# The order of seven products and their PSUM banks in a two-layer decoder trunk

## The chip, the cores and the metric

One core of a Trainium2 chip runs the whole program. The metric is the device time of one execution in microseconds; lower is better. TensorE (PE) multiplies, VectorE (DVE) and ScalarE (ACT) prepare its operands and read its results, SyncE (SP) issues plain loads from HBM, GpSimd (POOL) issues loads that add onto what is in SBUF.

## The reference

Two decoder layers over 256 tokens of width 2048, in float32. Each layer is a mixer and a feed-forward part:

```python
for layer in range(DEPTH):
    h = rms_norm(x, norm_mix[layer])
    x = x + (swa_ssd_mixer(h, ...) if layer % 2 == 0 else dilated_mixer(h, ...))
    h = rms_norm(x, norm_ffn[layer])
    x = x + squared_relu_mlp(h, w_up[layer], w_down[layer])

def squared_relu_mlp(h, w_up, w_down):
    u = jnp.einsum('bsd,df->bsf', h, w_up)
    return jnp.einsum('bsf,fd->bsd', jnp.square(jax.nn.relu(u)), w_down)
```

The change lies in the second product of the feed-forward part: `u` is 256 x 8192, `w_down` is 8192 x 2048, and there are two such layers.

## The kernel before

**Precision and pieces.** Each weight tile of 2 x 128 rows and 512 columns is loaded by SyncE, rounded into a high part by ScalarE (`whi`) and a low part by VectorE (`wlo`), and multiplied three times: activations high by weights high, high by low, low by high. The unit of the plan is a *piece*, one such tile. A piece of `w_up` is 12 matmuls of 512 columns, since both halves of the tokens (t = 0, 1) use it; a piece of the seven products is 6.

**The order of work** is a list of pieces, `plan`, which `run` walks. At piece i it issues the low part of piece i + 2, the load of piece i + 6, the high part of piece i + 3 and the weight sum of piece i + 4 (in this order), then the reads of the banks that the piece before has finished, then some steps of side tasks (norms, transposes, operands), and then piece i's matmuls. Every engine does its own instructions in the order in which they are issued. There are four buffers for low parts and five for high parts, so the low part of a piece waits until the piece four places back has left TensorE. Loads of `w_up` go through four tiles (`wraw`).

**Stages.** The 16 units of `w_up` (512 columns, 8 pieces each) come in order. Of `u`, 1024 columns make one stage c, 0 to 7. Stages 0 to 6 multiply by `w_down` in two *sets* of seven products each: set j = 0 makes output columns 0 to 1023, set j = 2 columns 1024 to 2047. Stage 7 is plain (`down`), four units of four pieces. `mixed` puts a stage's 28 product pieces between the pieces of `w_up` of the stages that follow: 18, 17, 17, 18, 17, 17 and 8 of them for stages 0 to 6. In stage 6 the first nine product pieces go with the last 8 pieces of `w_up`, the other 19 between the pieces of stage 7.

**The seven products.** A set takes a 2 x 2 block of token halves and `w_down` row halves by a 2 x 2 block of weights (names "11", "12", "21", "22": row half, column half) and computes it with 7 products instead of 8, as in Strassen's and Winograd's method. Each product has two pieces, h = 0 and 1. P1 and P2 use operands as they are (`uhl`, or `uh` and `ul`), the others sums of operands (`sh`, `sl`, `uh`). Their weights are a block or a sum of blocks:

- "12" is loaded with P1, and GpSimd's DMA adds block 22 onto it (`accumulate`); Q7 uses it.
- "11" is loaded with P1; when P1's low part is made, GpSimd's DMA adds block 12 onto it; Q5 uses it.
- "21" and "22" are loaded with P2; Q3 uses "22" as it is.
- Q6 uses the sum of "11" and "22", which VectorE adds into a tile of its own, "t2". Q4 uses "21" plus t2, added into the tile of "21".

The products of a set are added up in three PSUM banks, which come from a pool of four (`aux`, tile `sp`; the transposes and other small things use the same four): `a`, `b`, `c`. A later product on a bank adds onto the earlier ones, which is how the method shares its sums. After each product `evict` lets VectorE add or subtract the bank's content to or from a 128 x 512 block of the result, `res`. A product that adds onto a bank must wait until the read of the product before it on that bank has ended.

The lines: `SEVEN`, `LOADS` and `SUMS` at 238 to 241; `Seven.fetch` (load, L260), `Seven.add` (the sum), `Seven.accumulate` (L274), `Seven.evict`; `run` with its `low`, `high`, `add`, `fetch`. Since all vector, scalar and matmul operations go through one recording helper, the profile gives them line L71.

Of the kernel before, what the change touches and what calls it, by code (L numbers as in the profile page):

```python
# [11 lines left out]
OP = mybir.AluOpType  # L12
# [28 lines left out]
def trunk(ctx: ExitStack, tc: tile.TileContext, x, norm_mix, norm_ffn, w_up, w_down, ab_w_in, ab_q_norm,  # L41
# [33 lines left out]
    V, S, PE = Engine(nc.vector, "V", 90, 1.04), Engine(nc.scalar, "S", 240, 0.83), Engine(nc.tensor, "PE", 0, 0.84)  # L75
# [157 lines left out]
    def unit(*a, **k):  # L233
# [1 line left out]

    SEVEN = (("P1", "a", "11"), ("P2", "b", "21"), ("Q7", "c", "12"), ("Q6", "a", "t2"), ("Q5", "a", "11"),
             ("Q4", "c", "21"), ("Q3", "a", "22"))
    LOADS = {"P1": ("12", "11"), "P2": ("21", "22")}  # L240
    SUMS = {"Q6": ("t2", "11", "22"), "Q4": ("21", "21", "t2")}

    class Seven:

# [12 lines left out]
        def fetch(self, p, h):  # L257
            for b in LOADS.get(SEVEN[p][0], ()):
                r, c = self.rows[int(b[0]) - 1] + h * KC, self.c0 + (int(b[1]) - 1) * W
                nc.sync.dma_start(self.tile(b, h),  # L260
                                  self.w[r * 128:(r + KC) * 128, c:c + W].rearrange("(k p) c -> p k c", p=128))
                if b == "12":
                    self.accumulate("12", 1, h)

        def add(self, p, h):
            if SEVEN[p][0] in SUMS:
                o, x, y = SUMS[SEVEN[p][0]]
                x, y = self.raw[x, h], self.raw[y, h]
                V.tensor_tensor(self.raw[o, h] if o != "t2" else self.tile(o, h), x, y, op=OP.add)

        def accumulate(self, b, half, h):

# [5 lines left out]
        def source(self, p, h):  # L278
            return self.raw[SEVEN[p][2], h]

        def evict(self, p):

            name, b, _ = SEVEN[p]
            t, j, op = {"P1": (0, 0, OP.add), "P2": (0, 0, OP.add), "Q6": (1, 0, OP.add), "Q7": (1, 1, OP.subtract),
                        "Q5": (1, 1, OP.subtract), "Q4": (1, 0, OP.add), "Q3": (0, 1, OP.subtract)}[name]
            r = self.to[t][j]
            V.tensor_tensor(r, r, self.bank[b], op=op)
            if p == 6 and self.after is not None:
                self.after()

    def run():
# [60 lines left out]
        for i, (u, c) in enumerate(todo):  # L352
            if i:
                low(i + AHEAD - 1)
                fetch(i + AHEAD - 1 + RAW)
                high(i + AHEAD)
                add(i + AHEAD + 1)
# [4 lines left out]
            if isinstance(u, Seven):  # L362
                p, h = c
                name, b, _ = SEVEN[p]
                if p in u.needs and h == 0:
# [837 lines left out]
```

## Time and profile before

| | us |
|---|---|
| median of 3 runs | 2362.49 (2360.01 to 2366.78) |
| profiled execution | 2363.23, its span 2361.4 |
| busy PE / DVE / ACT / POOL | 2282.4 / 1794.7 / 1302.3 / 143.3 |
| mean granted clock of TensorE | 0.982 |
| moved by DMA | 483.49 MB, 205 GB/s in the mean |

The feed-forward stages with sets stand at about 535 to 1210 us and 1665 to 2355 us of the span. A view by stretches gives for each window of time the busy time of each engine, the number of its instructions (x), the clock that TensorE was granted (1.00 is full), the DMA engines' busy share and GB/s. A row of waits reads: engine, tile and line of the waiting instruction, whom it waited for, total us, times, longest us. A row of the timeline reads: start, length, engine, line, operation with its output and inputs, and in brackets the idle time ahead and what ended it. A matmul's length in the timeline (0.39 us) is its way through the array; back to back, they start 0.23 us apart.

### The profile page before, as it was taken

Reading aid. Unit: us, or ns where it says so; the run is one execution under the profiler, and the core shown is the slowest. Engines: PE = TensorE matmul, PEld = TensorE weight load, DVE = VectorE, ACT = ScalarE, POOL = GpSimd, SP = SyncE. Lnnn points to the kernel's source line nnn. Section 1 sums busy time; section 2 is a strip of 40 time slices with the busy share of each in tenths; the row PEclk is TensorE's granted clock in tenths of the full one; section 3 lists DMA queues with packets and bytes.
Section 4 is the critical chain, followed back from the end, with each engine's and each line's share of the span. In section 5 each row is a group of like instructions: output and inputs, shape, how many; then the busy total and the mean of one; then the engine's idle time right before and its main releaser. Section 6 shows DMA issues by size and latency. Waiting matters only on the chain.

```text
span 2361.4 us, 30348 instructions
## 1 busy us (share of the span) xinstructions
PE 2282.4 (97%) x10981; PEld 1886.5 (80%) x10981; DVE 1794.7 (76%) x2534; ACT 1302.3 (55%) x1639; POOL 143.3 (6%) x132
## 2 busy tenths in 40 slices
PE   8999999999999999999899999999999999999989
PEld 7999988887877877878688778778787787877867
DVE  6779886557887877978786767655687797877877
ACT  5565554445565655655565555554565565655654
POOL 1000000001001010011000000000101001101100
PEclk9999999999999999999999999999999999999999
DMA  7546555569778697697746555446879769688784
GB/s 228 165 137 195 177 177 187 187 198 274 191 229 252 196 273 208 193 294 202 225 147 191 160 160 170 156 160 186 254 203 278 205 198 270 198 245 240 207 248 125
DMA packets 259959, 483.49 MB, mean 205 GB/s; under 512 B 17444, under 2 KB 28240, under 8 KB 259808
## 3 DMA queue, kind: packets, MB, share of 16 engines
q1 hardware_dynamic: 219264, 416.34, 53.7%
q0 software_dynamic: 30976, 58.87, 14.0%
q10 hardware_dynamic: 9568, 6.34, 0.9%
q8 instruction: 86, 1.41, 0.2%
q14 instruction: 65, 0.53, 0.1%
HBM read 479.36 MB, written 2.13 MB: 204 GB/s over the span
## 4 chain that ended last, share of the span: by engine, by line
PE 79%; DMA 15%; DVE 3%; ACT 2%; issue 1%; SPq 0%; ACTq 0%; DVEq 0%
PE acc L71 55%; PE sp L71 19%; DMA wraw<-in_w_up_dram 11%; DMA sraw<-in_w_down_dram 4%; DVE wlo L71 1%; PE sc L71 1%; PE uT L71 1%; ACT whi L71 1%; PE o L71 1%; PE pT L71 1%; PE yp L71 1%; PE xT L71 0%; DMA wraw<-in_ab_w_in_dram 0%; DVE res L71 0%; DVE sraw L71 0%
## 5 line engine op out<-in xcount | busy, mean ns | idle before, releaser
L71 DVE TENSOR_TENSOR wlo<-wraw,whi 128x1024 fp32r<-128x1024 f32 (+1 forms) x568 | 687.8, 1215 | 259.8 <-PE acc L71 150.3
L71 ACT ACTIVATE whi<-wraw 128x1024 fp32r<-128x1024 f32 (+1 forms) x568 | 597.1, 1053 | 456.2 <-PE acc L71 273.8
L71 PE MATMUL acc<-whi,hThi 128*128 128x512 f32 (+1 forms) x1632 | 657.8, 403 | 21.2 <-ACT whi L71 19.7
L71 PE MATMUL acc<-wlo,hThi 128*128 128x512 f32 (+1 forms) x1632 | 644.8, 395 | 14.2 <-DVE wlo L71 14.0
L71 ACT ACTIVATE whi<-sraw 128x1024 fp32r<-128x1024 f32 x392 | 412.2, 1058 | 424.9 <-DVE sraw L71 137.5
L71 PE MATMUL acc<-whi,hTlo 128*128 128x512 f32 (+1 forms) x1632 | 642.9, 394 | 0.6 <-DVE hTlo L71 0.6
L71 DVE TENSOR_TENSOR wlo<-sraw,whi 128x1024 fp32r<-128x1024 f32 x392 | 476.1, 1223 | 128.7 <-ACT whi L71 65.7
L71 PEld LDWEIGHTS acc<-whi,hThi 128*128 128x128 f32 x1632 | 312.6, 192 | 91.2 <-ACT whi L71 23.8
L71 PEld LDWEIGHTS acc<-wlo,hThi 128*128 128x128 f32 x1632 | 313.0, 192 | 79.6 <-DVE wlo L71 18.6
L71 PEld LDWEIGHTS acc<-whi,hTlo 128*128 128x128 f32 x1632 | 312.8, 192 | 66.6 <-DVE hTlo L71 1.2
L274 POOL DMA_DIRECT2D sraw<-in_w_down_dram x112 | 134.8, 1204 | 2162.0 <-DMA sraw<-in_w_down_dram 1038.4
L71 PE MATMUL sp<-whi,sh 128*128 128x512 f32 x448 | 176.8, 395 | 8.7 <-DVE res L71 8.7
L71 PE MATMUL sp<-wlo,sh 128*128 128x512 f32 x448 | 176.4, 394 | 1.1 <-DVE wlo L71 1.1
L71 PE MATMUL sp<-whi,sl 128*128 128x512 f32 x448 | 176.1, 393 | 0.0
L71 DVE TENSOR_TENSOR res<-res,sp 128x512 f32<-128x512 f32 x196 | 134.1, 684 | 26.7 <-PE sp L71 26.4
L71 DVE TENSOR_TENSOR sraw<-sraw 128x1024 f32<-128x1024 f32 x112 | 136.7, 1220 | 0.0
L71 PE MATMUL acc<-hThi,whi 128*128 128x256 f32 x384 | 112.4, 293 | 0.0
L71 PE MATMUL acc<-hThi,wlo 128*128 128x256 f32 x384 | 108.6, 283 | 0.0
L71 PE MATMUL acc<-hTlo,whi 128*128 128x256 f32 x384 | 108.5, 283 | 0.0
L71 PEld LDWEIGHTS sp<-whi,sh 128*128 128x128 f32 x448 | 85.7, 191 | 28.1 <-ACT whi L71 9.1
L71 PEld LDWEIGHTS sp<-wlo,sh 128*128 128x128 f32 x448 | 85.4, 191 | 19.8 <-DVE wlo L71 1.9
L71 PEld LDWEIGHTS sp<-whi,sl 128*128 128x128 f32 x448 | 85.2, 190 | 18.0
(227 smaller groups left out, 2708.6 us busy)
## 6 DMA issues: line engine op xcount, KB each, us to landing
wraw<-in_w_up_dram SPq DMA_DIRECT2D x256, 512.0 KB, 5.1
sraw<-in_w_down_dram SPq DMA_DIRECT2D x224, 512.0 KB, 8.8
sraw<-in_w_down_dram POOLq DMA_DIRECT2D x112, 512.0 KB, 9.9
wraw<-in_ab_w_in_dram SPq DMA_DIRECT2D x96, 512.0 KB, 3.7
wraw<-in_c_w_qkv_dram SPq DMA_DIRECT2D x96, 512.0 KB, 4.1
wraw<-in_ab_w_out_dram SPq DMA_DIRECT2D x48, 512.0 KB, 3.5
wraw<-in_w_down_dram SPq DMA_DIRECT2D x32, 512.0 KB, 4.3
wraw<-in_c_w_o_dram SPq DMA_DIRECT2D x32, 512.0 KB, 3.5
```

The source lines that it names most:

```text
L71: return f(out, *a, **k)
L274: nc.gpsimd.dma_start(self.raw[b, h], self.w[r * 128:(r + KC) * 128, c:c + W].rearrange("(k p) c -> p k c", p=128), accum_op=OP.add)
```

## The change

Q3 moves from the seventh place to the third, and gets a bank `d` of its own. The order was P1, P2, Q7, Q6, Q5, Q4, Q3 and is P1, P2, Q3, Q7, Q6, Q5, Q4. Because Q3 no longer adds onto bank `a`, Q5's content of `a` is now read twice, into two blocks of `res`. And since "22" has been used by then, the sum for Q6 is written into the tile of "22" instead of a tile of its own; Q4's sum reads it there.

```diff
-    SEVEN = (("P1", "a", "11"), ("P2", "b", "21"), ("Q7", "c", "12"), ("Q6", "a", "t2"), ("Q5", "a", "11"),
-             ("Q4", "c", "21"), ("Q3", "a", "22"))
+    SEVEN = (("P1", "a", "11"), ("P2", "b", "21"), ("Q3", "d", "22"), ("Q7", "c", "12"), ("Q6", "a", "22"),
+             ("Q5", "a", "11"), ("Q4", "c", "21"))
     LOADS = {"P1": ("12", "11"), "P2": ("21", "22")}
-    SUMS = {"Q6": ("t2", "11", "22"), "Q4": ("21", "21", "t2")}
+    SUMS = {"Q6": ("22", "11", "22"), "Q4": ("21", "21", "22")}
...
-                V.tensor_tensor(self.raw[o, h] if o != "t2" else self.tile(o, h), x, y, op=OP.add)
+                V.tensor_tensor(self.raw[o, h], x, y, op=OP.add)
...
-            t, j, op = {"P1": (0, 0, OP.add), "P2": (0, 0, OP.add), "Q6": (1, 0, OP.add), "Q7": (1, 1, OP.subtract),
-                        "Q5": (1, 1, OP.subtract), "Q4": (1, 0, OP.add), "Q3": (0, 1, OP.subtract)}[name]
-            r = self.to[t][j]
-            V.tensor_tensor(r, r, self.bank[b], op=op)
+            for t, j, op in {"P1": ((0, 0, OP.add),), "P2": ((0, 0, OP.add),), "Q6": ((1, 0, OP.add),),
+                             "Q7": ((1, 1, OP.subtract),), "Q4": ((1, 0, OP.add),), "Q3": ((0, 1, OP.subtract),),
+                             "Q5": ((1, 1, OP.subtract), (0, 1, OP.subtract))}[name]:
+                r = self.to[t][j]
+                V.tensor_tensor(r, r, self.bank[b], op=op)
```

How the order of instructions moves, at three places. TensorE, layer 0, stage 1, first set, where the fifth product ends and the sixth begins with no piece of `w_up` between them (`sp_` with a number is one bank's tile, `whi` and `wlo` the weights' parts, `sh` and `sl` or `uh` and `ul` the operands). Before, Q5's last three matmuls and Q4's first three:

```order
L71 MATMUL sp_6111<-whi_6255,sh_6068 128x512
L71 MATMUL sp_6111<-wlo_6264,sh_6068 128x512
L71 MATMUL sp_6111<-whi_6255,sl_6069 128x512
L71 MATMUL sp_6200<-whi_6266,uh_6017 128x512
L71 MATMUL sp_6200<-wlo_6287,uh_6017 128x512
L71 MATMUL sp_6200<-whi_6266,ul_6018 128x512
```

Now, Q6's last three and Q5's first three:

```order
L71 MATMUL sp_6111<-whi_6254,sh_6068 128x512
L71 MATMUL sp_6111<-wlo_6262,sh_6068 128x512
L71 MATMUL sp_6111<-whi_6254,sl_6069 128x512
L71 MATMUL sp_6111<-whi_6264,sh_6068 128x512
L71 MATMUL sp_6111<-wlo_6285,sh_6068 128x512
L71 MATMUL sp_6111<-whi_6264,sl_6069 128x512
```

Both products now write the same bank, and the read of the first lies between them.

VectorE at the same place (`wlo<-sraw` is a product piece's low part, `wlo<-wraw` that of a piece of `w_up`, `sraw<-sraw` a sum of blocks, `res<-res,sp` the read of a bank). Before, up to Q5's read of `sp_6111`:

```order
L71 TENSOR_TENSOR wlo_6253<-sraw_5970,whi_6245 128x1024
L71 TENSOR_TENSOR sraw_6035<-sraw_6035,sraw_6174 128x1024
L71 TENSOR_TENSOR wlo_6264<-sraw_5985,whi_6255 128x1024
L71 TENSOR_TENSOR res_82<-res_82,sp_6111 128x512
L71 TENSOR_TENSOR wlo_6287<-sraw_6035,whi_6266 128x1024
L71 TENSOR_TENSOR sraw_6062<-sraw_6062,sraw_6198 128x1024
L71 TENSOR_TENSOR wlo_6300<-wraw_6243,whi_6291 128x1024
L71 TENSOR_TENSOR wlo_6310<-sraw_6062,whi_6302 128x1024
L71 TENSOR_TENSOR res_82<-res_82,sp_6111 128x512
```

Now, up to Q6's read of `sp_6111`:

```order
L71 TENSOR_TENSOR wlo_6262<-sraw_6064,whi_6254 128x1024
L71 TENSOR_TENSOR res_82<-res_82,sp_6245 128x512
L71 TENSOR_TENSOR wlo_6285<-sraw_5970,whi_6264 128x1024
L71 TENSOR_TENSOR wlo_6297<-wraw_6240,whi_6289 128x1024
L71 TENSOR_TENSOR sraw_6035<-sraw_6035,sraw_6037 128x1024
L71 TENSOR_TENSOR wlo_6308<-sraw_5985,whi_6299 128x1024
L71 TENSOR_TENSOR res_82<-res_82,sp_6111 128x512
```

Ahead of the last read there were a low part, a sum, a low part of `w_up` and a low part; now the sum stands behind the low part of `w_up`.

TensorE, layer 0, stage 6, first set, where several product pieces follow each other. Before, the end of Q6's second piece and the beginning of Q5's first, on one bank:

```order
L71 MATMUL sp_9700<-whi_9820,sh_9671 128x512
L71 MATMUL sp_9700<-wlo_9829,sh_9671 128x512
L71 MATMUL sp_9700<-whi_9820,sl_9672 128x512
L71 MATMUL sp_9700<-whi_9831,sh_9671 128x512
L71 MATMUL sp_9700<-wlo_9839,sh_9671 128x512
L71 MATMUL sp_9700<-whi_9831,sl_9672 128x512
```

Now, the same place in the row of pieces, the end of Q7's second piece and the beginning of Q6's first:

```order
L71 MATMUL sp_9844<-whi_9816,sh_9673 128x512
L71 MATMUL sp_9844<-wlo_9826,sh_9673 128x512
L71 MATMUL sp_9844<-whi_9816,sl_9674 128x512
L71 MATMUL sp_9700<-whi_9828,sh_9671 128x512
L71 MATMUL sp_9700<-wlo_9837,sh_9671 128x512
L71 MATMUL sp_9700<-whi_9828,sl_9672 128x512
```

Q6 and Q5 are parted there by a piece of stage 7 now, and the two products that touch are on two banks.

## The prediction

> **What bounds the kernel now.** I read the shares of the engines first, then the stretches of 60 us, then the waits of TensorE, then the timeline at the places of the waits. Of the page:
>
> ```profile
> PE 2282.4 (97%) x10981; PEld 1886.5 (80%) x10981; DVE 1794.7 (76%) x2534; ACT 1302.3 (55%) x1639; POOL 143.3 (6%) x132
> ```
>
> TensorE is busy for 97% of the span, so what a change can win is its 79 us of idle time (2361.4 - 2282.4) and what goes with it. The view of stretches says where that lies (length, then busy time and instructions of each engine, the granted clock, the DMA share, GB/s):
>
> ```profile
> 660.00:720.00 60.00, 60.00 (x274) 49.70 (x273) 53.92 (x53) 37.48 (x40) 4.82 (x4) 1.00 0.68 191
> 720.00:780.00 60.00, 55.93 (x232) 44.70 (x231) 45.89 (x46) 32.00 (x35) 8.42 (x7) 0.91 0.97 288
> 1260.00:1320.00 60.00, 60.00 (x299) 47.64 (x298) 38.60 (x104) 32.21 (x46) 0.00 (x0) 1.00 0.52 166
> ```
>
> Outside the feed-forward stages TensorE never stops. Inside them full stretches alternate with stretches in which the DMA engines are 97% busy, TensorE loses 4 us and its clock falls. So TensorE is the bound everywhere, and once in each stage the loads are. The timeline of stage 2's first set (start, length, engine, operation; in brackets the idle time before it and what ended it):
>
> ```profile
> 743.80 1.06 ACT L71 ACTIVATE whi<-sraw 128x1024 fp32r<-128x1024 f32 x1 [6.93 <-DMA sraw<-in_w_down_dram]
> 744.91 0.73 PE L71 MATMUL sp<-whi,uh 128*128 128x512 f32 x1 [2.06 <-ACT whi L71]
> 746.17 0.79 PE L71 MATMUL sp<-wlo,uh 128*128 128x512 f32 x1 [0.53 <-DVE wlo L71]
> 748.35 1.06 ACT L71 ACTIVATE whi<-wraw 128x1024 fp32r<-128x1024 f32 x1 [3.50 <-DMA wraw<-in_w_up_dram]
> ```
>
> The matmul that waits has `uh` as its operand: of the first two products that is P2, the second. ScalarE waits for P2's second weight tile, and then for the next tile of `w_up`, which stands behind it in SyncE's queue. The same pair of waits stands once in every stage, at P2 and the `w_up` piece behind it. Of the waits of TensorE:
>
> ```profile
> PE acc L71 <- ACT whi L71: 19.7, 8, 3.8
> PE acc L71 <- DVE wlo L71: 14.0, 11, 4.0
> PE sp L71 <- DVE res L71: 8.7, 3, 4.2
> PE sp L71 <- DVE wlo L71: 7.9, 13, 0.8
> PE sp L71 <- ACT whi L71: 7.4, 4, 2.8
> ```
>
> The third row is the one that this change touches: a product that adds onto a bank waits until VectorE has read the product before it out of that bank.
>
> **The change part by part.** The loads first. P1 and P2 stay in front, they fetch the same tiles at the same pieces, and the accumulating DMAs are issued at the same pieces: SyncE's and GpSimd's queues hold the same transfers in the same order. So the pair of waits at P2 stays, and I count nothing for it. What is won is time for the sums, and that nobody waited for:
>
> ```profile
> L71 DVE TENSOR_TENSOR sraw<-sraw 128x1024 f32<-128x1024 f32 x112 | 136.7, 1220 | 0.0
> L71 DVE TENSOR_TENSOR res<-res,sp 128x512 f32<-128x512 f32 x196 | 134.1, 684 | 26.7 <-PE sp L71 26.4
> ```
>
> The 112 sums had 0.0 us of idle time before them, so the accumulated tiles had always landed. Their number and size stay; only the tile that they write is another.
>
> Each set reads a bank once more, since Q3's block now takes Q5's bank too: 28 x 0.684 = 19 us more of VectorE. It hides: in the full stretch 660 to 720 VectorE is busy 53.92 of 60 us, which leaves 6.1 us where some 1.4 sets add about 1 us. Were VectorE the bound for all of the sets, it would cost the 19 us. The fourth bank comes from the same four buffers as before; Q3's bank is free again after its one read, at most two banks are held for long, as before, and I count nothing.
>
> The order of the banks is what costs. Bank `a` takes P1, Q6, Q5 and then Q3 before, and P1, Q6, Q5 now. Q6 and Q5 follow each other in both. What parts them is the plan: a unit of `w_up` (12 matmuls) mostly stands between two products, but in stages 1, 2, 4 and 5 the fifth and sixth product of the first set touch. Before these were Q5 and Q4, on banks `a` and `c`; now they are Q6 and Q5, both on `a`. The instructions of TensorE show it as 18 matmuls in a row on one bank, four times a layer, and in stage 6's second set the same pair touches once more: 10 new places. What leaves is the pair in stage 6's first set, 24 matmuls in a row, once a layer.
>
> What one new place costs is read where the fifth product ends today, in stage 1 (DVE from 669, PE's first matmul of the fifth product's two pieces and of the sixth):
>
> ```profile
> 670.74 1.22 DVE L71 TENSOR_TENSOR wlo<-sraw,whi 128x1024 fp32r<-128x1024 f32 x1
> 671.88 1.22 DVE L71 TENSOR_TENSOR sraw<-sraw 128x1024 f32<-128x1024 f32 x1
> 672.38 0.39 PE L71 MATMUL sp<-whi,sh 128*128 128x512 f32 x1
> 673.01 1.22 DVE L71 TENSOR_TENSOR wlo<-wraw,whi 128x1024 fp32r<-128x1024 f32 x1
> 673.74 0.39 PE L71 MATMUL sp<-whi,sh 128*128 128x512 f32 x1
> 674.31 1.22 DVE L71 TENSOR_TENSOR wlo<-sraw,whi 128x1024 fp32r<-128x1024 f32 x1
> 675.10 0.39 PE L71 MATMUL sp<-whi,uh 128*128 128x512 f32 x1
> 675.45 0.68 DVE L71 TENSOR_TENSOR res<-res,sp 128x512 f32<-128x512 f32 x1
> ```
>
> The read of the bank ended at 676.13 (675.45 + 0.68), and the next product began at 675.10. On one bank it would have begun 0.14 us behind the read (that gap is in the stage 6 rows below), at 676.27: a wait of 1.2 us. Now one sum moves. Before it stood ahead of the `w_up` piece's low part (671.88); in the changed order it stands behind it. That low part can't begin before TensorE is through with the `w_up` piece four pieces back, at about 672.55 (its last matmul, one spacing of 0.23 before 672.38, lasts 0.39), for there are four buffers. So: low part 672.55, sum 1.14 later at 673.7, low part at 674.8, the read at 675.95 to 676.64, the next product at 676.8. That is 1.7 us behind 675.10. The eight such places cost 13.6 us. In stage 6's second set the low part and the sum both stand between the release and the read, with 6 matmuls instead of 12 to cover them: the unit ahead is through, then 1.14 + 1.14 + 0.69 + 0.14 = 3.1 us with 1.2 us of matmuls, a wait of 2.0 us, twice: 4.0 us. Behind the waiting matmul stands all of TensorE's work, nothing overtakes it. The wait's bounds: 1.2 us if the sum finds a gap, 5.9 us (4.2 and a half-clock stretch) if VectorE is as far behind as in stage 6. I take the worked value, for at 675 VectorE was not behind. The ten together: 17.6 us, between 12 and 59.
>
> Stage 6's first set, as it is now:
>
> ```profile
> 1126.99 1.22 DVE L71 TENSOR_TENSOR wlo<-sraw,whi 128x1024 fp32r<-128x1024 f32 x1
> 1129.75 0.39 PE L71 MATMUL sp<-whi,sh 128*128 128x512 f32 x1
> 1135.80 0.39 PE L71 MATMUL sp<-whi,sl 128*128 128x512 f32 x1
> 1139.53 0.69 DVE L71 TENSOR_TENSOR res<-res,sp 128x512 f32<-128x512 f32 x1
> 1140.36 0.47 PE L71 MATMUL sp<-whi,sh 128*128 128x512 f32 x1 [4.18 <-DVE res L71]
> 1143.81 1.25 ACT L71 ACTIVATE relu<-acc,rs 128x512 f32<-128x512 f32 x2
> 1147.77 0.79 PE L71 MATMUL acc<-whi,uh 128*128 128x512 f32 x1 [1.68 <-ACT uh L71]
> ```
>
> (1139.53 + 0.69 = 1140.22, and TensorE went on at 1140.36: the 0.14.) Six pieces run here without a unit between them, and the wait of 4.18 us lies inside. The changed set puts Q3, Q7 and Q6 there, on three banks, so that wait goes. What is late next is VectorE itself: six low parts, two sums and two reads from 1126.99 on, 8 x 1.14 + 2 x 0.6 = 10.3, so the last low part is done at 1137.3, and TensorE ends the six pieces at about 1138.4 instead of 1144.8 (1140.36 and the 12 matmuls that were left, 8 of them at half clock). Then the first piece of the last stage needs `uh`, whose chain starts with ScalarE's `relu`. That stands behind a high part which waits for a buffer of the first Q6 piece, leaves TensorE at 1137, and has two more ahead of it: `relu` at about 1139.5. From `relu` to the first matmul it took 3.96 us (1147.77 - 1143.81), so 1143.4 instead of 1147.77: 4.3 us won a layer, 8.6 in all, between 0 (the chain starts where it does now) and 11.8 (the wait and its half-clock stretch, both layers).
>
> Sum: 13.6 + 4.0 - 8.6 = +9.0 us on the profiled execution's 2363.23 us, 2372.2. The median of the runs shown is 0.7 us below that execution, so I say 2371.
>
> [...] The stretches around such waits (660.50 to 664 and 1152 to 1156 are full speed for comparison):
>
> ```profile
> 655.50:659.00 3.50, 3.04 (x7) 2.09 (x7) 3.50 (x4) 3.50 (x5) 0.00 (x0) 0.50 0.61 170
> 660.50:664.00 3.50, 3.50 (x19) 2.90 (x19) 3.43 (x4) 1.69 (x3) 1.20 (x1) 1.00 0.87 273
> 1140.90:1144.30 3.40, 3.40 (x10) 2.62 (x9) 2.75 (x3) 1.45 (x2) 0.00 (x0) 0.51 0.86 260
> 1148.50:1151.00 2.50, 2.46 (x7) 1.58 (x6) 2.50 (x3) 1.11 (x2) 0.00 (x0) 0.50 0.98 262
> ```
>
> Behind the waits of 2.19 us (655), 4.18 us (1140) and 1.68 us (1147, with short transposes ahead of it) the clock is half for some 3.4 us, which costs 1.7 us. Behind two waits just before the first of them it was not:
>
> ```profile
> 651.55 0.50 PE L71 MATMUL sp<-wlo,uh 128*128 128x512 f32 x1 [0.76 <-DVE wlo L71]
> 651.88 0.40 PE L71 MATMUL sp<-whi,ul 128*128 128x512 f32 x1
> 652.12 0.39 PE L71 MATMUL sp<-whi,uh 128*128 128x512 f32 x1
> ```
>
> There the matmuls go on at the full spacing of 0.23 us. A new wait of 1.7 us between dense matmuls lies between these rows, and I count no half clock. [...]
>
> **The rivals.**
>
> No net change, 2363 (0.26): VectorE has its sums done early, each new wait is the 1.2 us of the row at 675.45 (12), and stage 6 wins all of its wait and the half-clock stretch (11.8). For it: VectorE has idle time in these stretches. Against: the sum stands behind the low part by the order of instructions.
>
> The half clock follows each new wait, 2388 (0.12): 10 x 1.7 on top. For it the row at 1147.77, against it 651.55.
>
> Faster, 2354 (0.13): ScalarE's waits for `sraw` are for the accumulated tile, which needs a load and an accumulating DMA one after the other, and Q7 now comes a product later, so that TensorE's waits for `sp` on high and low parts (7.4 + 7.9 = 15.3) and a half-clock stretch or so (1.7) go: 2371 - 17. It decides if the matmul that waits has Q7's operand `sh`. Against it: at 744.91 it is `uh`, and the sums' idle time of 0.0.
>
> Slower by far, above 2390 (0.04): VectorE is as far behind at the new places as in stage 6.
>
> **How the numbers follow.** The forecast has 0.45, with 2364 to 2379 as its own range. About 0.3%, 7 us, is what a measurement of this kernel tells from no change: below 2355.4 is faster, above 2369.6 slower. Of the forecast's 0.45 I put 0.30 above that bound, 0.13 within and 0.02 below; of the first rival 0.24 within and the rest halved; the third is faster but for a sliver, the others slower. So faster 0.16, same 0.37, slower 0.47. The range, 2355 to 2388, runs from the edge of the faster rival to the half-clock one.
>
> **What would show it.** TensorE's waits of `sp` for `res` grow from 8.7 us in 3 to about 18 us in 10 or so, each near 1.7, none near 4.2; the matmul that waits has `sh` and stands in stages 1, 2, 4 and 5. The wait at stage 6's first set is gone, and the last stage's first matmul stands some 4 us nearer to that set's begin. The reads of banks go from 196 to 224 and VectorE's busy time up by 19 us, the sums stay 112. The waits at P2, its second tile and then `w_up`, are where they were and as long. I am wrong if those shrink, if a wait of TensorE appears at a new bank or at a sum, or if the granted clock falls behind the new waits.

## The result, and the profile after

The changed kernel takes 2387.44 us (median of 4 runs, 2386.23 to 2389.18), the kernel before beside it 2362.39 (2360.01 to 2366.78). The ratio is 1.0104, with a 95% interval of 1.0087 to 1.0122: slower by 25 us. The forecast was 2371 in a range of 2355 to 2388, so its sign was right, the time lies within a microsecond of the range's upper end, and of the 25 us the sum had 9.

The changed kernel's page: the shares of the engines, then the bank reads and the sums among its groups.

```profile
PE 2288.7 (96%) x10981; PEld 1888.1 (79%) x10981; DVE 1812.0 (76%) x2562; ACT 1303.2 (55%) x1639; POOL 143.4 (6%) x132
...
L71 DVE TENSOR_TENSOR res<-res,sp 128x512 f32<-128x512 f32 x224 | 150.7, 683 | 22.3 <-PE sp L71 21.7
...
L71 DVE TENSOR_TENSOR sraw<-sraw 128x1024 f32<-128x1024 f32 x112 | 136.6, 1220 | 0.0
```

The span is 2386.3 us against 2361.4. TensorE's idle time grew from 79.0 to 97.6 us (2386.3 - 2288.7), and its busy time by 6.3: the same 10981 matmuls, at a mean granted clock of 0.979 instead of 0.982. VectorE reads 224 banks and still has a quarter of the span free; no wait of TensorE is put down to a sum. The waits of TensorE (total, times, longest):

```profile
PE acc L71 <- ACT whi L71: 19.8, 9, 3.1
PE sp L71 <- ACT whi L71: 16.5, 10, 3.4
PE sp L71 <- DVE res L71: 16.2, 10, 2.7
PE acc L71 <- DVE wlo L71: 13.3, 11, 4.0
PE sp L71 <- DVE wlo L71: 7.6, 10, 0.8
PE uT L71 <- ACT relu L71: 7.0, 6, 4.6
```

Two rows grew by much. `sp <- res` went from 8.7 us in 3 to 16.2 in 10, as forecast. `sp <- whi` went from 7.4 in 4 to 16.5 in 10, which was not forecast at all: these are the waits at P2.

**The touching bank.** The timeline of VectorE and TensorE in stage 1's first set, at the place that the prediction worked through:

```profile
675.05 1.22 DVE L71 TENSOR_TENSOR wlo<-wraw,whi 128x1024 fp32r<-128x1024 f32 x1 [1.06 <-issue]
676.19 1.22 DVE L71 TENSOR_TENSOR sraw<-sraw 128x1024 f32<-128x1024 f32 x1
677.33 1.22 DVE L71 TENSOR_TENSOR wlo<-sraw,whi 128x1024 fp32r<-128x1024 f32 x1
678.46 0.68 DVE L71 TENSOR_TENSOR res<-res,sp 128x512 f32<-128x512 f32 x1
679.29 0.47 PE L71 MATMUL sp<-whi,sh 128*128 128x512 f32 x1 [1.39 <-DVE res L71]
```

This is the forecast's chain: the low part of `w_up` when its buffer comes free, then the sum, a low part, the read, and the matmul 4.24 us behind the first of them (worked out: 4.25). Eight such waits stand in stages 1, 2, 4 and 5. Idle time is 1.39 us; from one product's first matmul to the next the segment grew by 1.55 us and the one behind it by 0.1.

**Set by set.** I measured both traces from the first matmul of P1 (operand `uhl`) to the first of the next set's P1, and inside a set from product to product:

| where | before, us | after, us | difference, all such sets | forecast |
|---|---|---|---|---|
| second sets of stages 0 to 5 | 47.2 to 50.4 | the same | 0 | 0 |
| fifth and sixth product of the first sets, stages 1, 2, 4, 5 | 2.72 + 5.44 | 4.27 + 5.53 | 8 x 1.64 = +13.1 | +13.6 |
| stage 6, second set (with what follows) | 518.27, 48.73 | 522.76, 51.40 | +7.2 | +4.0 |
| stage 6, first set | 55.17, 57.19 | 51.81, 52.26 | -8.3 | -8.6 |
| P1 and P2 of the first sets, stages 1 to 5 | 18.73 (mean) | 19.88 (mean) | 10 x 1.15 = +11.5 | 0 |

The rows add up to 23.5 of the 24.9 us by which the span grew (2386.3 - 2361.4); the other 1.4 lie in the first set of the first layer's stage 0 (46.29 to 47.71). The last row is the open question with which the experiments began: SyncE and GpSimd have the same transfers in the same order, the second sets didn't move by a tenth, and yet P2 waits longer in the first sets.

### The profile page after: what moved, and what is told of

It is laid out like the page before. It is cut to its first block, busy times and chain, and to the rows that moved or that the text cites. A ratio compares the mean times of both kernels' runs of the same rounds, so it can differ in the third digit from the quotient of the medians.

```text
span 2386.3 us, 30315 instructions
## 1 busy us (share of the span) xinstructions
PE 2288.7 (96%) x10981; PEld 1888.1 (79%) x10981; DVE 1812.0 (76%) x2562; ACT 1303.2 (55%) x1639; POOL 143.4 (6%) x132
## 4 chain that ended last, share of the span: by engine, by line
PE 78%; DMA 15%; DVE 3%; ACT 2%; issue 1%; SPq 0%; ACTq 0%; DVEq 0%
PE acc L71 55%; PE sp L71 18%; DMA wraw<-in_w_up_dram 12%; DMA sraw<-in_w_down_dram 2%; DVE wlo L71 2%; ACT whi L71 1%; PE uT L71 1%; PE sc L71 1%; PE o L71 1%; PE pT L71 1%; DVE res L71 1%; PE yp L71 1%; DVE sraw L71 0%; PE xT L71 0%; DMA wraw<-in_ab_w_in_dram 0%
## 5 line engine op out<-in xcount | busy, mean ns | idle before, releaser
L71 PE MATMUL sp<-whi,sh 128*128 128x512 f32 x448 | 176.7, 394 | 16.2 <-DVE res L71 16.2
L71 DVE TENSOR_TENSOR res<-res,sp 128x512 f32<-128x512 f32 x224 | 150.7, 683 | 22.3 <-PE sp L71 21.7
L71 PE MATMUL sp<-whi,uh 128*128 128x512 f32 x224 | 89.2, 398 | 16.5 <-ACT whi L71 16.5
L71 PEld LDWEIGHTS sp<-wlo,sh 128*128 128x128 f32 x448 | 85.1, 190 | 17.6
```

Source lines behind the costliest of these rows:

```text
L71: return f(out, *a, **k)
```

## The experiments

**e1_parted, the touching bank undone.** Q6 goes ahead of Q7, so that Q7 stands between Q6 and Q5.

```diff
-    SEVEN = (("P1", "a", "11"), ("P2", "b", "21"), ("Q3", "d", "22"), ("Q7", "c", "12"), ("Q6", "a", "22"),
+    SEVEN = (("P1", "a", "11"), ("P2", "b", "21"), ("Q3", "d", "22"), ("Q6", "a", "22"), ("Q7", "c", "12"),
              ("Q5", "a", "11"), ("Q4", "c", "21"))
```

> The changed kernel with the fourth and fifth product exchanged (P1, P2, Q3, Q6, Q7, Q5, Q4 on banks a, b, d, a, c, a, c), so that Q6 and Q5 on bank a are parted by Q7 everywhere. Theory A, the touching bank is the cause of its ten waits and the longer waits at P2 have a cause of their own: TensorE's waits of sp for res fall from 16.2 us in 10 to under 1, the ten segments lose 12.3 + 5.4 = 17.7 us, and the first sets keep their longer waits at P2: about 2370. Theory B, the longer waits at P2 follow from the ten waits: those shrink too, about 14 us more, and the kernel ends below the one before, near 2355.

It took 2365.59 us, a ratio to the kernel before of 1.0004 (0.9994 to 1.0013). No wait of `sp` for `res` is left, but this is:

```profile
PE acc L71 <- ACT whi L71: 16.1, 9, 3.9
...
PE sp L71 <- ACT whi L71: 14.3, 8, 3.7
```

Theory A: without the ten places, which had 13.1 + 7.2 = 20.3 us in the table, the kernel is 22 us faster than the changed one, and P2's waits stay (P1 and P2 take 19.90 us on the mean). They are no consequence of the bank waits.

**e2_own_tile, the tiles' places.** The sum for Q6 takes a tile of its own again.

```diff
-    SEVEN = (("P1", "a", "11"), ("P2", "b", "21"), ("Q3", "d", "22"), ("Q7", "c", "12"), ("Q6", "a", "22"),
+    SEVEN = (("P1", "a", "11"), ("P2", "b", "21"), ("Q3", "d", "22"), ("Q7", "c", "12"), ("Q6", "a", "t2"),
...
-    SUMS = {"Q6": ("22", "11", "22"), "Q4": ("21", "21", "22")}
+    SUMS = {"Q6": ("t2", "11", "22"), "Q4": ("21", "21", "t2")}
...
-                V.tensor_tensor(self.raw[o, h], x, y, op=OP.add)
+                V.tensor_tensor(self.raw[o, h] if o != "t2" else self.tile(o, h), x, y, op=OP.add)
```

> The changed kernel, but the sum for Q6 goes into a tile of its own again (and Q4's sum reads it), so that each set takes ten tiles of the work pool instead of eight, as before. Theory A, the place of the tiles plays no part: as the changed kernel, 2387, with the longer waits at P2. Theory C, what moved the loads at P2 is where the tiles lie: the first sets' stretch to the third product goes back to what it was before, about 14 us less, 2373, with the ten bank waits unchanged.

2389.47 us, a ratio of 1.0103 (1.0086 to 1.0120); P1 and P2 take 19.86 us. Which tile the sum writes plays no part.

**e3_before_double, the added reads alone**, and **e4_before_again, chance.** The order of before, with Q3 in bank `d` at the end and Q5's bank read twice; and the kernel before once more.

```diff
-             ("Q4", "c", "21"), ("Q3", "a", "22"))
+             ("Q4", "c", "21"), ("Q3", "d", "22"))
...
-                        "Q5": (1, 1, OP.subtract), "Q4": (1, 0, OP.add), "Q3": (0, 1, OP.subtract)}[name]
...
+                             "Q5": ((1, 1, OP.subtract), (0, 1, OP.subtract))}[name]:
```

> The kernel before, its order kept, with the third product's block in a bank of its own at the end and the fifth product's bank read twice: the added reads and the fourth bank alone. Theory A, they hide: 2362 (within 4), VectorE's busy time up by 19 us, no new wait of TensorE. Theory D, VectorE's added reads delay the weights' parts at P2: the first sets' stretch to the third product grows by about 1 us each, 2376.

> The kernel before, unchanged, profiled once more: how much the stretch from the first to the third product varies from one execution to the next. If the growth of about 1 us in each first set is chance, this execution shows such differences against the first one too, in sum up to 14 us; if not, the sum of the 14 differences stays within 3 us.

e3 took 2367.51 us, a ratio of 1.0015 (1.0005 to 1.0024): the 28 added reads (16.6 us more of VectorE's time in the changed kernel, 150.7 - 134.1) and the fourth bank cost 3.7 us. P1 and P2 take 18.74 us in it. e4 is one execution, of 2369.05 us, and its P1 and P2 take 18.99 us against 18.73 in the first profile. Over all 14 first sets it differs by 7.3 us in sum, more than the 3 that its expectation allows, half of it in one set of stage 6; in the ten sets of the table it differs by 2.7, the changed kernel by 11.5. Three kernels with the new order stand at 19.86 to 19.90 and three executions with the old one at 18.73 to 18.99, so the growth is not chance, and it comes neither from the bank nor from the reads as such. What the three kernels with the longer P2 share is the order, and that each set ends with Q4, which needs a sum; before, Q3 was last, which needs none.

**What stands at a set's end.** The timeline of VectorE and of SyncE's queue in the kernel before, where stage 0's second set ends (the next set begins at 642.37):

```profile
619.71 2.57 DVE L71 TENSOR_TENSOR wlo<-sraw,whi 128x1024 fp32r<-128x1024 f32 x2
622.59 0.69 DVE L71 TENSOR_TENSOR res<-res,sp 128x512 f32<-128x512 f32 x1 [0.31 <-PE sp L71]
623.19 1.22 DVE L71 TENSOR_TENSOR wlo<-wraw,whi 128x1024 fp32r<-128x1024 f32 x1
...
624.86 2.19 SPq L260 DMA_DIRECT2D sraw<-in_w_down_dram  x4
```

The same place in the changed kernel (the next set begins at 643.84):

```profile
621.09 1.22 DVE L71 TENSOR_TENSOR sraw<-sraw 128x1024 f32<-128x1024 f32 x1
622.23 2.52 DVE L71 TENSOR_TENSOR wlo<-sraw,whi 128x1024 fp32r<-128x1024 f32 x2
624.67 1.28 DVE L71 TENSOR_TENSOR res<-res,sp 128x512 f32<-128x512 f32 x2
625.86 3.80 DVE L71 TENSOR_TENSOR wlo<-wraw,whi 128x1024 fp32r<-128x1024 f32 x3
...
627.53 2.39 SPq L260 DMA_DIRECT2D sraw<-in_w_down_dram  x4
```

The low part of `w_up` (`wlo<-wraw`) frees one of the four buffers of `w_up`'s tiles. SyncE's queue holds a load of `w_up` that waits for it, and the four loads for P1 stand behind that load; in both kernels they go out 1.67 us behind the begin of that low part. Such waits fill most of the queue's time, as its longest row of waits in the kernel before shows (L306 issues the loads of `w_up` and of the other plain weights):

```profile
SPq L306 <- DVE wlo L71: 1611.6, 484, 12.4
```

Before, the loads for P1 went out 642.37 - 624.86 = 17.51 us ahead of the set; now, with Q4's sum (1.14 us) and Q5's second read (0.60) ahead of that low part and VectorE without a gap there, 643.84 - 627.53 = 16.31 us. The queue has the same order, and all of it is 1.2 us late.

**e5_q5_last, no sum at the set's end.** Q4 and Q5 exchanged. This also parts Q6 from Q5.

```diff
-             ("Q5", "a", "11"), ("Q4", "c", "21"))
+             ("Q4", "c", "21"), ("Q5", "a", "11"))
```

> The changed kernel with the sixth and seventh product exchanged: P1, P2, Q3, Q7, Q6, Q4, Q5 on banks a, b, d, c, a, c, a. Q6 and Q5 are parted by Q4, and the last product of a set needs no sum, as before. Theory V, the longer waits at P2 come from VectorE's sum at the set's end (it makes the low part of w_up late, which frees the buffer for which SyncE's queue waits ahead of the loads of P1 and P2): the ten waits go and the first sets' stretch of P2 falls back by 1.1 us each, about 2355 (e1_parted's 2365.6 less 11). Theory L, Q3's place behind P2 makes them longer, whatever stands at the end: as e1_parted, 2366.

The place of the two kernels above, in this one (the next set begins at 643.38):

```profile
621.68 2.36 DVE L71 TENSOR_TENSOR wlo<-sraw,whi 128x1024 fp32r<-128x1024 f32 x2
623.96 0.68 DVE L71 TENSOR_TENSOR res<-res,sp 128x512 f32<-128x512 f32 x1
624.55 1.22 DVE L71 TENSOR_TENSOR wlo<-wraw,whi 128x1024 fp32r<-128x1024 f32 x1
...
626.22 2.32 SPq L260 DMA_DIRECT2D sraw<-in_w_down_dram  x4
```

The loads go out 17.16 us ahead, and P1 and P2 take 18.88 us on the mean, within the spread of the kernel before. So theory V holds for P2, although Q3 is in third place as in e1. The time, 2372.57 us, a ratio of 1.0033 (1.0020 to 1.0046), misses the expected 2355, because stage 6's first set became 57.7 and 58.0 us long instead of 51.4 and 51.7 (e1). Its timeline:

```profile
1143.11 1.06 ACT L71 ACTIVATE whi<-sraw 128x1024 fp32r<-128x1024 f32 x1 [2.00 <-DVE sraw L71]
1144.08 1.25 ACT L71 ACTIVATE relu<-acc,rs 128x512 f32<-128x512 f32 x2
1144.80 2.34 PE L71 MATMUL uT<-cst,relu 128*128 128x128 f32 x8 [5.46 <-ACT relu L71]
```

There the last stage's `relu` stands on ScalarE behind high parts that now wait for Q4's sum on VectorE, and TensorE waits 5.46 us. The order that is good for stages 1 to 5 is bad for stage 6. This explains 12.6 of the 17.6 us; the rest is in single sets, the largest of them P2 of the second layer's stage 0 (14.98 us against 12.48 in e1), and stays open.

**e6_q3_last, the order of before without stage 6's bank wait.**

```diff
-    SEVEN = (("P1", "a", "11"), ("P2", "b", "21"), ("Q7", "c", "12"), ("Q6", "a", "t2"), ("Q5", "a", "11"),
-             ("Q4", "c", "21"), ("Q3", "d", "22"))
+    SEVEN = (("P1", "a", "11"), ("P2", "b", "21"), ("Q7", "c", "12"), ("Q6", "a", "t2"), ("Q4", "c", "21"),
+             ("Q5", "a", "11"), ("Q3", "d", "22"))
```

(The edit is against e3.)

> The kernel before with the sum's own tile, Q3 still last in a bank of its own (Q5's bank read twice), and Q5 and Q4 exchanged: P1, P2, Q7, Q6, Q4, Q5, Q3 on banks a, b, c, a, c, a, d. The bank theory: the 4.18 us waits in stage 6's first set go (about 5 us a layer) and no new one comes, P2 stays as before: about 2354 to 2357. Rival, VectorE itself is late there and the time only moves to its low parts: 2362 to 2364.

2368.00 us, a ratio of 1.0012 (1.0003 to 1.0021). Stage 6's first set is 53.2 and 54.0 us, some 2 to 3 less than before rather than 5. P1 and P2 take 19.03 us, 0.3 more, hardly beyond the spread of the kernel before: here Q5's two reads stand ahead of the low part that frees `w_up`'s buffer, without a sum. Nothing is won, and the time lies above what either theory had; the rival is closer.

**e7_sum_sooner**, each sum issued one piece earlier, and **e8_read_first**, the reads issued ahead of the next pieces' work.

```diff
-                add(i + AHEAD + 1)
+                add(i + AHEAD + 2)
```

```diff
+            for f in pending:
+                f()
+            pending = []
             if i:
                 low(i + AHEAD - 1)
...
-            for f in pending:
-                f()
-            pending = []
```

> The changed kernel with each sum issued one piece earlier. If VectorE's queue ahead of the read sets the new waits, they shrink where the sum leaves that place, from 1.39 towards 0.8 us, 8 x 0.5 = 4 us, and at the set's end the sum that stands ahead of w_up's low part goes up one place, so that part of P2's growth (up to 11 us) comes back: 2373 to 2383. If the wait is the read's own time and the queue plays no part: 2387.

> The changed kernel with the reads of finished banks issued ahead of the next pieces' low part and sum on VectorE. The shortest wait is then the read itself, 0.69 us, and the gaps around it, about 0.8 in place of 1.39 and of 2.4 to 2.7: 8 x 0.6 + 2 x 1.8 and a half-clock stretch, some 10 us less, 2377, if nothing else is late. Rival: VectorE now stands behind the end of each product with the low parts behind it, w_up's buffers come free later, P2's waits and those of acc for wlo grow: 2387 or more.

e7 took 2392.78 us, a ratio of 1.0123 (1.0108 to 1.0139), and e8 2398.11, a ratio of 1.0145 (1.0128 to 1.0162). e8 is slower than the change (1.0087 to 1.0122); for e7 the intervals overlap, and it lies outside both of its expectations. In e7 P1 and P2 fell to 19.35 us, so 0.5 of the 1.15 came back, but sums now stand right ahead of reads for which TensorE waits:

```profile
968.13 1.22 DVE L71 TENSOR_TENSOR sraw<-sraw 128x1024 f32<-128x1024 f32 x1
969.27 0.68 DVE L71 TENSOR_TENSOR res<-res,sp 128x512 f32<-128x512 f32 x1
...
970.09 0.47 PE L71 MATMUL sp<-whi,sh 128*128 128x512 f32 x1 [1.84 <-DVE res L71]
```

In e8 the bank waits shrank, and those at P2 grew by more:

```profile
PE sp L71 <- ACT whi L71: 27.9, 10, 4.8
...
PE sp L71 <- DVE res L71: 11.8, 10, 1.4
```

P1 and P2 take 21.03 us in it: VectorE now waits for the end of the product with the low part of `w_up` behind it. The rival held. Both runs say the same of VectorE: what stands ahead of the read makes the bank late, and what stands ahead of `w_up`'s low part makes the loads late.

How far ahead of its set P1's first load goes out can be read in every trace. The mean of the ten sets is 16.95 us in both profiles of the kernel before and 16.93 in e3, but 15.83 in the changed kernel, 15.94 in e1, 15.83 in e2, 16.69 in e5, 16.35 in e6, 16.28 in e7 and 14.57 in e8. Added to the length of P1 and P2 it gives 35.4 to 35.9 us in each of them: what the loads lose, TensorE loses. It also parts the two causes. The second read alone (e6) makes the loads 0.60 us late, its own length; the changed kernel's are 1.12 late, so the other 0.5 are left for Q4's sum.

**e10_after_raw5 and e11_before_raw5, an older low part for SyncE's queue to wait for.** A fifth buffer for `w_up`'s tiles, in the changed kernel and in the one before, paid for with one of the 31 tiles of the work pool. Every load is also issued a piece earlier; no run has the one without the other.

```diff
-RAW = 4
+RAW = 5
-    work = ctx.enter_context(tc.tile_pool(name="work", bufs=31))
+    work = ctx.enter_context(tc.tile_pool(name="work", bufs=30))
```

> The changed kernel with five buffers for w_up's tiles instead of four (and 30 instead of 31 tiles in the work pool), so that SyncE's queue doesn't wait for the newest of VectorE's low parts and every load goes out a piece earlier. Theory V (P2's growth is the late release of w_up's buffer): TensorE's waits at P2 shrink, and the changed kernel has no more growth there than the kernel before with the same buffer: the two differ by the bank waits less stage 6, about 12 us, instead of 24. The ten bank waits stay. If the loads are bound by the DMA engines alone, nothing moves: 2387.

> The kernel before with the same fifth buffer for w_up's tiles and 30 work tiles: what the buffer alone brings, to be compared with e10_after_raw5. Theory V: its stretch of P1 and P2 shrinks by less than that of the changed kernel, 0 to 1 us a set, 2353 to 2363. If the DMA engines bind: 2363.

2288.45 us, a ratio to the kernel before of 0.9680 (0.9662 to 0.9699), and 2276.28, a ratio of 0.9627 (0.9606 to 0.9649). That is far more than either theory had for the kernel before: P2's waits in stages 1 to 5 are not shorter, they are gone: P1 and P2 take 11.5 and 11.4 us on the mean. So no growth at P2 is left between the two kernels, as theory V had it. They differ by 12.2 us instead of 25, and that this is theory V's 12 is luck in part: the eight touching places have 16.0 us here, stage 6 has 7.2 - 4.9, and 5.2 come back because e11, unlike e10, waits at P2 of the second layer's stage 0. The page and the waits of e10:

```profile
PE 2246.1 (98%) x10981; PEld 1868.0 (82%) x10981; DVE 1810.8 (79%) x2562; ACT 1304.6 (57%) x1639; POOL 143.4 (6%) x132
...
PE sp L71 <- DVE res L71: 19.2, 10, 2.7
```

The ten bank waits are still there; the rows of `sp` and `acc` for `whi`, 36 us together in the changed kernel, are gone. In stage 1 the loads for P1 now go out 639.53 - 617.32 = 22.2 us ahead of the set, again 1.66 us behind the begin of a low part of `w_up`, but of the one before:

```profile
615.66 1.22 DVE L71 TENSOR_TENSOR wlo<-wraw,whi 128x1024 fp32r<-128x1024 f32 x1
...
617.32 2.28 SPq L260 DMA_DIRECT2D sraw<-in_w_down_dram  x4
```

The 20 us ahead of that set and the 20 us behind its begin, in the kernel before (two rows) and in e10 (two rows):

```profile
622.37:642.37 20.00, 20.00 (x93) 16.61 (x92) 17.24 (x18) 12.79 (x14) 4.55 (x4) 1.00 0.89 262
642.37:662.37 20.00, 15.63 (x58) 11.57 (x57) 10.27 (x10) 7.16 (x8) 0.42 (x2) 0.83 0.98 292
```

```profile
619.53:639.53 20.00, 20.00 (x93) 16.61 (x92) 18.65 (x20) 13.40 (x15) 4.55 (x4) 1.00 1.06 331
639.53:659.53 20.00, 20.00 (x94) 16.60 (x93) 17.42 (x17) 12.98 (x14) 2.67 (x3) 1.00 1.07 332
```

The last two columns are the DMA share and GB/s. A share of 0.89 and 0.98 was read as a full DMA, but with one more buffer the same engines move 331 GB/s in the same place, and TensorE doesn't stop. Means of 20 us hide what happens; stretches of 3 us, in the kernel before (two rows) and in e10 (three rows), show it:

```profile
624.37:627.37 3.00, 3.00 (x15) 2.48 (x14) 1.67 (x3) 1.49 (x3) 0.00 (x0) 1.00 0.63 152
639.37:642.37 3.00, 3.00 (x14) 2.46 (x14) 2.66 (x3) 1.06 (x1) 0.94 (x1) 1.00 1.10 261
```

```profile
618.53:621.53 3.00, 3.00 (x17) 2.50 (x16) 2.92 (x4) 2.94 (x4) 0.00 (x0) 1.00 0.92 315
630.53:633.53 3.00, 3.00 (x15) 2.49 (x14) 2.96 (x6) 1.96 (x2) 0.00 (x0) 1.00 1.10 263
636.53:639.53 3.00, 3.00 (x14) 2.46 (x14) 2.67 (x3) 1.06 (x1) 0.94 (x1) 1.00 1.07 403
```

From 636 to 651 us the kernel before has a share of 1.09 to 1.10 at 260 to 264 GB/s, and e10 has the same share and rate while TensorE runs on. So within the burst of loads the DMA engines are full in both, as far as the share tells. What differs is when the burst begins: in the kernel before the engines are still at 0.63 and 152 GB/s 18 to 15 us ahead of the set; e10 is at 0.92 and 315 GB/s already 21 to 18 us ahead. The slow stretch is the one in which GpSimd's accumulating transfers land, 4 us apart; in it P2's four loads land 4 us apart too (at -1.3, 2.8, 6.7 and 10.3 us from the set's begin), those of P1 just ahead of it 1.4. That the accumulating transfers are its cause is not shown, since no run leaves them out.

**e9_two_orders and e12_two_orders_raw5, a version that beats both.** e5's order in the stages 0 to 5, e1's in stage 6; then the same with the fifth buffer.

```diff
+    LATE = (("P1", "a", "11"), ("P2", "b", "21"), ("Q3", "d", "22"), ("Q6", "a", "22"), ("Q7", "c", "12"),
+            ("Q5", "a", "11"), ("Q4", "c", "21"))
...
+            self.order = SEVEN if after is None else LATE
```

> The changed kernel with two orders: P1, P2, Q3, Q7, Q6, Q4, Q5 (as e5_q5_last) in the stages 0 to 5, and P1, P2, Q3, Q6, Q7, Q5, Q4 (as e1_parted) in stage 6. If the account holds (ten bank waits, VectorE's sum at the set's end in stages 1 to 5, stage 6's first set): no bank wait, P1 to the end of P2 at 18.8 us on the mean of stages 1 to 5, as before and in e5_q5_last, and stage 6's first set at 51.5 as in e1_parted against 55 to 57 before: e1_parted's 2365.6 less 10 x 1.2, 2354, faster than both kernels. If the time comes back elsewhere: 2362 or more.

> e9_two_orders with the fifth buffer for w_up's tiles and 30 work tiles. With P2's waits gone, the order should still win what it wins without them: no wait of sp for res (5.8 us in e11_before_raw5), stage 6's first set at 47.1 to 48.4 as in e10_after_raw5 against 49.4 to 51.0, and, if e10's short P2 in the second layer's stage 0 comes from the order, 5 us there: 2276.3 less 5 to 12, 2264 to 2271. If the fifth buffer makes the order worthless: 2276, as e11_before_raw5.

e9: 2360.21 us, a ratio of 0.9985 (0.9975 to 0.9995), 3.4 us better than before and 27 better than the change, but 6 short of the expected 2354. P1 and P2 take 18.92 us in stages 1 to 5 and stage 6's first set 51.1 and 52.2, as expected; in the profiled execution stage 0's two first sets took 3.3 us back. e12: 2269.89 us, a ratio of 0.9601 (0.9587 to 0.9614), below e11's 0.9627, and the intervals overlap (e11's begins at 0.9606), so the two orders are only likely to be worth their 6 us there.

## Why the prediction was right, and where it was wrong

*The eight touching places, forecast 13.6 us.* Right: 13.1. The chain of five instructions was where and as long as worked out. e1 shows that the bank is the cause: parted by Q7, the waits are gone.

*Stage 6's second set, forecast 4.0 us.* Mis-sized: 7.2. VectorE and TensorE there, in the changed kernel:

```profile
1208.39 1.22 DVE L71 TENSOR_TENSOR wlo<-wraw,whi 128x1024 fp32r<-128x1024 f32 x1
1209.53 1.28 DVE L71 TENSOR_TENSOR res<-acc,res 128x512 f32<-128x512 f32 x2
1210.72 1.21 DVE L71 TENSOR_TENSOR wlo<-sraw,whi 128x1024 fp32r<-128x1024 f32 x1
1211.86 1.22 DVE L71 TENSOR_TENSOR sraw<-sraw 128x1024 f32<-128x1024 f32 x1
1212.99 0.68 DVE L71 TENSOR_TENSOR res<-res,sp 128x512 f32<-128x512 f32 x1
1213.82 0.47 PE L71 MATMUL sp<-whi,sh 128*128 128x512 f32 x1 [2.69 <-DVE res L71]
```

The sum counted a low part and a sum ahead of the read. It left out the two reads of `acc` of the last stage's unit (1.28 us), which stand there too. In the first layer a half-clock stretch came on top (a granted clock of 0.61 over 1214 to 1218 us, where the sixth product took 9.88 instead of 8.16 us).

*Stage 6's first set, forecast -8.6 us.* Right for the set as a whole, -8.3, with some luck: behind P2, which is what the forecast was about, the two sets lost 11.8 us against this profile of the kernel before and 8.2 against its second one (e4), and P1 and P2 grew by 3.5 there, which is no more than they vary in stage 6 of the unchanged kernel (3.7 in one set). And the gain hangs on more than the bank: with the banks parted, e5's order lost it again through ScalarE's `relu`.

*The 28 added reads and the fourth bank, forecast 0.* Too low: e3 has them alone and is 3.7 us slower, with an interval of 1.2 to 5.7 (0.0005 and 0.0024 of 2364), and where the second read stands ahead of `w_up`'s low part it makes P1's loads 0.60 us late in each set (e6). The prediction asked only whether VectorE has room for them.

*No half clock behind the new waits.* Right for those of 1.39 us: the stretch behind the first has a granted clock of 1.00 (the first of the three rows in the last section), and the product behind each of the eight takes 5.53 or 5.54 us, 0.1 more than before. The rival at 2388 came within a microsecond of the measured time, but for another reason. That the time lies inside the range is luck: with its own terms as measured, 13.1 + 7.2 - 8.3 = 12.0, the sum would give 2363.2 + 12.0 = 2375, and the range reaches up to 2388 only for the half clock that did not come.

*"SyncE's and GpSimd's queues hold the same transfers in the same order. So the pair of waits at P2 stays, and I count nothing for it."* This step failed. P1 and P2 of the ten first sets grew by 11.5 us, the largest part of the 16 that the sum did not have. The order of a queue says what goes out, and not when. The question not asked was what the queue waits for just ahead of P1's loads: a buffer of `w_up`, which VectorE frees, and on VectorE the change put a sum and a read ahead of that. The prediction asked what stands behind a waiting matmul on TensorE, and not what stands behind a waiting load on SyncE. e3 rules out the reads where they stand earlier in the set, e4 chance, e2 the tiles, e1 the bank; e5 shows that with neither a sum nor a second read at the set's end the growth goes, and e10 that it goes when the queue waits for the low part before that one and its loads go out 5 to 6 us sooner. Of the 1.12 us by which P1's loads are late, the second read has 0.60 (e6) and the sum the rest.

*"What is won is time for the sums, and that nobody waited for."* Misread, without harm here: the 0.0 us of idle time ahead of the sums says that the sums did not wait. ScalarE's high parts did wait for sums, 137.5 us in 86 waits, but no wait of TensorE is put down to one.

*"... and once in each stage the loads are [the bound]."* Half right. Within the burst of loads the DMA engines were full as far as the share tells (1.10 at 260 GB/s), but that the burst began so late was not theirs: just ahead of it they were at 0.63. This was in the profile, where the waits stood once in each stage at the same place. The fifth buffer, with the earlier issue that it allows, bears that out, with 87 us for the kernel before (2363.60 - 2276.28).

## What to carry to other kernels

Where a change puts work on an engine that also frees buffers, follow the freed buffer to the queue that waits for it, and what stands behind it there: a microsecond on an engine with a quarter of its time free cost a microsecond of TensorE in each of the stages 1 to 5 (the loads went out 1.12 us later, P1 and P2 took 1.15 us longer). A busy DMA share beside a stall that returns at the same place in each stage (0.89 and 0.98 here) doesn't show that the loads could not have come in time: with a fifth buffer and the earlier issue they did. Look at the share just ahead of the stall (0.63 here), and let one more buffer start them sooner. And one order for all stages has to be checked in each kind of stage, since the order that took the sum off the end of stages 1 to 5 put it ahead of a `relu` in stage 6 (a wait of 5.46 us).

## What the runs showed of the hardware

The half clock doesn't follow the length of a wait alone. The stretches behind three new waits of the changed kernel, of 1.39, 2.69 and 2.38 us (the granted clock is the third number from the end):

```profile
679.40:683.40 4.00, 4.00 (x18) 3.32 (x19) 3.15 (x3) 1.19 (x2) 0.00 (x0) 1.00 1.02 372
...
1214.00:1218.00 4.00, 4.00 (x12) 3.15 (x12) 3.80 (x5) 2.04 (x4) 0.00 (x0) 0.61 0.44 128
2365.70:2369.70 4.00, 4.00 (x18) 3.29 (x19) 3.30 (x3) 1.44 (x2) 0.00 (x0) 1.00 0.01 4
```

The wait of 2.69 us was followed by half clock (0.50 from 1215.0 to 1218.2 us) and that of 2.38 was not, while in e7 the wait of 1.84 us, shown above, had slow matmuls behind it from 971.64 us on, among them:

```profile
971.64 0.63 PE L71 MATMUL acc<-whi,hThi 128*128 128x512 f32 x1
972.07 0.63 PE L71 MATMUL acc<-wlo,hThi 128*128 128x512 f32 x1
```

They start 0.43 us apart, as at half clock in the kernel before (657.02 and 657.45), and from 974.96 on 0.23 again. The half clock that the prediction put behind the wait of 2.19 us (655.17) began with that wait: the granted clock was 1.00 up to 652.8 us and 0.50 from 653.0 to 659.5, and the wait began at 655.17 - 2.19 = 652.98, behind waits of 0.95 and 0.76 us. No run here tells what decides beside the length of a wait, or where a limit lies.

The DMA share does not tell the rate: within one burst of e10 it is 1.10 at 263 GB/s and 1.07 at 403 GB/s.
